# Attention scores on one core: three hand-kept 32 KB buffers in place of a rotating tile pool

## The chip, the core and the metric

The kernel runs on one core of a Trainium2 chip. The metric is the device time of one execution in microseconds, lower is better.

## The reference

```python
batch, heads, seq, dim = 8, 8, 512, 64          # q, k: float32
scale = 1.0 / np.sqrt(q.shape[-1])
out = (np.einsum('bhqd,bhkd->bhqk', q, k) * scale).astype(np.float32)
```

16.78 MB go in, 67.11 MB come out, and the arithmetic between is small.

## The kernel before

The work is cut into four units of two batches. Each unit loads k and q as fp32 into one 32 KB-per-partition tile (two loads of 2.1 MB), GpSimd casts them to bf16, TensorE transposes them, and VectorE and ScalarE copy the transposes to `kT` and `qz`. Then four output tiles per unit follow: sixteen matmuls into PSUM, eight evictions of 128 x 1024 with the scale (`n_evac % 6` deals them out, half to each engine), and one store of 4.2 MB. Input tiles and output tiles come from the same pool of three.

```python
    big_pool = ctx.enter_context(tc.tile_pool(name="big", bufs=3))
    ...
    def evacuate(dst, src):
        nonlocal n_evac

        if n_evac % 6 in (0, 2, 3):
            pinned(nc.scalar.mul(out=dst, in_=src, mul=scale))
        else:
            pinned(nc.vector.tensor_scalar(out=dst, in0=src, scalar1=scale, scalar2=None,
                                           op0=mybir.AluOpType.mult))
        n_evac += 1
    ...
    def load_and_cast(v):

        xf = big_pool.tile([P, 2, 2, J * D], f32, name="big")
        both = []
        for x, src in enumerate((k_r, q_r)):
            nc.sync.dma_start(out=xf[:, x], in_=src[v].rearrange("p (s c) -> p s c", s=2))
        for x in range(2):
            xb = bf_pool.tile([P, J, 2, D], bf16, name="xb")
            for s in range(2):
                pinned(nc.gpsimd.tensor_copy(out=xb[:, :, s, :],
                                             in_=xf[:, x, s].rearrange("p (j d) -> p j d", j=J)))
            both.append(xb)
        return both
    ...
    def scores(v, t):

        kT, qz = ts[v]
        o = big_pool.tile([P, 2, RO, S], f32, name="big")
        for x in range(2):
            n = 2 * t + x
            for i in range(0, RO, 2):
                ps = psum_pool.tile([P, 2, S], f32, name="ps")
                for w in range(2):
                    pinned(nc.tensor.matmul(out=ps[:, w, :], lhsT=qz[:, i + w, n, :],
                                            rhs=kT[:, n].rearrange("d m s j -> d (m s j)"),
                                            start=True, stop=True))
                evacuate(o[:, x, i:i + 2, :], ps)
                yield
        nc.sync.dma_start(out=out_r[v, t], in_=o.rearrange("p x i k -> p x (i k)"))
```

(Cuts are marked with `...`; the transposes, their copies and the main loop, which interleaves the transposes of the next unit with the scores of this one, are left out.)

## Time and profile before

| | before |
|---|---|
| time, median of three runs | 203.24 us (202.83 to 203.37) |
| span of the profiled run | 201.3 us |
| VectorE, ScalarE, TensorE busy | 126.4, 100.7, 99.2 us |
| DMA queue, share of 16 engines | 98.1% |
| moved | 83.89 MB |

(In the lines of profiles, PE is TensorE, DVE VectorE, ACT ScalarE, POOL GpSimd, and SP the engine that issues the DMAs; a q behind a name is that engine's sequencer, under which the waits stand, as with the 33 event semaphores of VectorE quoted below.)

The table answers one question: is any resource full? Only the DMA is. VectorE is busy 63% of the time, and the longest of its waits is for the queue: evictions waited 29.1 us on VectorE and 30.8 us on ScalarE for old stores to land. So the idle columns of the groups matter less here than the row of DMA shares. Two things are not on the page and had to be worked out from the trace: when each store is issued, and how many bytes stand in the queue at that moment (bytes issued before, less bytes moved). The second is called the backlog below. It is the time by which a store may be late before the DMA starves: the same 7.35 us of delay cost 5.5 us where the backlog was 3.2 us and 0.4 us where it was 9.3 us, as the second experiment shows.

### The profile page before, as it was taken

The numbers are of one execution on the slowest core, as the hardware profiler recorded it, in microseconds if no ns is written. First come the engines' busy times: TensorE is split into PE (matmuls) and PEld (weight loads), VectorE is DVE, ScalarE is ACT, GpSimd is POOL, SyncE is SP. The second block draws the span as 40 slices with busy tenths as digits, with TensorE's granted clock in tenths as the row PEclk, the third lists the DMA queues.
The fourth block names the chain that finished last, engine by engine and source line by source line (L and its number), as shares of the span: only waits on it lengthen the run. The fifth ranks groups of instructions, "written<-read, shape, count | busy, mean of one in ns | idle before, by whom it ended". The sixth has DMA issues, their size and how long they took to land.

```text
span 201.3 us, 1456 instructions
## 1 busy us (share of the span) xinstructions
PE 99.2 (49%) x503; PEld 48.3 (24%) x512; DVE 126.4 (63%) x130; ACT 100.7 (50%) x129; POOL 30.6 (15%) x22
## 2 busy tenths in 40 slices
PE   0033366753976729463729554856535666710000
PEld 0033353321522414231315221432212222200000
DVE  6726659995989929796749796569635264530000
ACT  2016667786674856583837663856515341510000
POOL 1277777556000000000000000000000000000000
PEclk9999999998599996999975998888995857555555
DMA  6999999999999999999999999999999999999993
GB/s 205 430 443 430 420 433 440 420 407 427 433 436 425 422 443 427 430 423 440 430 423 433 433 430 427 440 430 423 433 436 430 410 446 433 420 423 433 433 427 163
DMA packets 5510, 83.97 MB, mean 417 GB/s; under 512 B 384, under 2 KB 384, under 8 KB 384
## 3 DMA queue, kind: packets, MB, share of 16 engines
q1 hardware_dynamic: 5504, 83.89, 98.1%
q8 instruction: 4, 0.07, 0.1%
q14 instruction: 2, 0.02, 0.0%
HBM read 16.78 MB, written 67.11 MB: 417 GB/s over the span
## 4 chain that ended last, share of the span: by engine, by line
DMA 63%; DVE 16%; PE 3%; POOL 3%; ACT 1%; POOLq 1%; issue 1%; SPq 0%; DVEq 0%; ACTq 0%
DMA out_dram<-big 43%; DMA big<-in_q_dram 20%; DVE big L66 12%; PE ps L132 3%; DVE qz L95 3%; POOL xb L82 3%; DVE kT L95 1%; ACT big L64 1%; POOLq L186 1%; SPq L78 0%; DVEq L66 0%; SPq L137 0%; ACTq L64 0%; POOLq L82 0%
## 5 line engine op out<-in xcount | busy, mean ns | idle before, releaser
L132 PE MATMUL ps<-kT,qz 128*128 128x512 bf16 x247 | 81.1, 450 | 55.1 <-ACT big L64 39.2
L66 DVE TENSOR_SCALAR big<-ps 128x1024 f32<-128x1024 f32 x64 | 76.3, 1222 | 39.9 <-DMA out_dram<-big 29.1
L64 ACT ACTIVATE big<-ps 128x1024 f32<-128x1024 f32 x64 | 63.7, 1023 | 57.0 <-DMA out_dram<-big 30.8
L132 PEld LDWEIGHTS <-qz 128*128 128x128 bf16 x256 | 27.5, 111 | 96.0 <-issue 83.2
L82 POOL CAST xb<-big 128x2048 bf16<-128x2048 f32 x16 | 29.9, 1896 | 17.6 <-DMA big<-in_k_dram 11.9
L95 DVE COPY kT<-tp 64x512 bf16<-64x512 bf16 x32 | 22.0, 687 | 6.3 <-PE tp L107 5.7
L95 ACT COPY kT<-tp 64x512 bf16<-64x512 bf16 x32 | 18.5, 578 | 14.7 <-PE tp L107 14.4
L95 DVE COPY qz<-tp 64x512 bf16<-64x512 bf16 x32 | 22.0, 687 | 3.1 <-PE tp L116 2.7
L95 ACT COPY qz<-tp 64x512 bf16<-64x512 bf16 x32 | 18.5, 578 | 3.9 <-PE tp L116 3.6
L107 PE MATMUL tp<-identity,xb 128*128 128x128 bf16 x128 | 12.0, 254 | 16.5 <-POOL xb L82 12.5
L116 PE MATMUL tp<-identity,xb 128*128 128x128 bf16 x128 | 12.8, 265 | 6.0 <-DVE kT L95 3.5
L107 PEld LDWEIGHTS <-xb 128*128 128x128 bf16 x128 | 10.5, 116 | 20.8 <-POOL xb L82 12.8
L116 PEld LDWEIGHTS <-xb 128*128 128x128 bf16 x128 | 11.3, 122 | 10.9 <-issue 8.9
L147 DVE MEMSET qz<- 128x4096 uint32 x2 | 6.9, 3472 | 2.5 <-PEq L175 1.7
L95 ACT ACT_TABLE_LOAD x1 | 1.3, 1283 | 0.7 <-PEq L175 0.7
masks.py:199 POOL TENSOR_SCALAR_AFFINE_SELECT identity<-identity 128x128 bf16<-128x128 bf16 x1 | 0.3, 294 | 0.1
masks.py:197 POOL MEMSET identity<- 128x128 bf16 x1 | 0.2, 205 | 0.3 <-POOLq L175 0.3
L175 POOL MEMSET const-float32-0.0<- 128x1 f32 x1 | 0.1, 99 | 0.2 <-issue 0.2
L175 POOL MEMSET const-bfloat16-1.0<- 128x1 bf16 x1 | 0.1, 102 | 0.0
L175 POOL MEMSET const-uint8-127<- 128x1 uint8 x1 | 0.1, 102 | 0.0
L175 POOL MEMSET const-float32-1.0<- 128x1 f32 x1 | 0.1, 99 | 0.0
## 6 DMA issues: line engine op xcount, KB each, us to landing
out_dram<-big SPq DMA_DIRECT2D x16, 4096.0 KB, 21.4
big<-in_k_dram SPq DMA_DIRECT2D x4, 2048.0 KB, 19.2
big<-in_q_dram SPq DMA_DIRECT2D x4, 2048.0 KB, 24.2
```

The costliest lines, as they stand in the source:

```text
L64: pinned(nc.scalar.mul(out=dst, in_=src, mul=scale))
L66: pinned(nc.vector.tensor_scalar(out=dst, in0=src, scalar1=scale, scalar2=None, op0=mybir.AluOpType.mult))
L82: pinned(nc.gpsimd.tensor_copy(out=xb[:, :, s, :], in_=xf[:, x, s].rearrange("p (j d) -> p j d", j=J)))
L95: pinned(copy(out=dst(s, h), in_=src[:, h]))
L107: pinned(nc.tensor.transpose(out=tp[:, j, :], identity=identity, in_=kb[:, j0 + j].rearrange("p s d -> p (s d)")))
L116: pinned(nc.tensor.transpose(out=tp[:, i, jj, :], identity=identity, in_=qb[:, RO * jj + i0 + i].rearrange("p s d -> p (s d)")))
L132: pinned(nc.tensor.matmul(out=ps[:, w, :], lhsT=qz[:, i + w, n, :], rhs=kT[:, n].rearrange("d m s j -> d (m s j)"), start=True, stop=True))
L147: nc.vector.memset(qz, 0.0)
L175: nc = _bacc.Bacc("TRN2", target_bir_lowering=False, num_devices=1)
L186: with _tile.TileContext(nc) as tc:
```

## The change

The intent was to drop the pool's bookkeeping: three persistent buffers are taken once and handed out in turn. What changes with it is the grain of the waits. A tile of a pool waits until the whole earlier tile is done with; a persistent buffer is tracked by overlapping bytes, and has a history for each of them.

```diff
-    big_pool = ctx.enter_context(tc.tile_pool(name="big", bufs=3))
...
+    n_big = 0
+
+    def next_big():
+
+        nonlocal n_big
+        n_big += 1
+        return bigs[(n_big - 1) % 3]
+
     def load_and_cast(v):
 
-        xf = big_pool.tile([P, 2, 2, J * D], f32, name="big")
+        xf = next_big().rearrange("p (x s c) -> p x s c", x=2, s=2)
...
-        o = big_pool.tile([P, 2, RO, S], f32, name="big")
+        o = next_big().rearrange("p (x i k) -> p x i k", x=2, i=RO)
...
+    bigs = [consts.tile([P, 2 * RO * S], f32, name=f"big{n}") for n in range(3)]
     cast = [load_and_cast(v) for v in range(UNITS)]
```

## The prediction

> **What bounds the kernel now.** I read the page of the kernel before from the top: busy shares, slices, DMA queues, chain, groups. Then I asked for the timeline of the issuing engine and for the windows. First the busy shares and the slices (tenths of each of 40 slices of about 5 us):
>
> ```profile
> PE 99.2 (49%) x503; PEld 48.3 (24%) x512; DVE 126.4 (63%) x130; ACT 100.7 (50%) x129; POOL 30.6 (15%) x22
> ...
> DMA  6999999999999999999999999999999999999993
> GB/s 205 430 443 430 420 433 440 420 407 427 433 436 425 422 443 427 430 423 440 430 423 433 433 430 427 440 430 423 433 436 430 410 446 433 420 423 433 433 427 163
> ```
>
> No compute engine is above 63%. The DMA row is 9 in every slice but the first and the last, and the rate sits between 407 and 446 GB/s throughout. The part on DMA queues says the same in one number:
>
> ```profile
> q1 hardware_dynamic: 5504, 83.89, 98.1%
> ```
>
> One queue carries 83.89 MB (16.78 read, 67.11 written), and its packets fill 98.1% of the 16 engines' span of 201.3 us: 197.5 us. So 3.8 us per engine is all that better feeding of the DMA could ever return, and most of that is the ramp of the first slice and the drain of the last. Reading the packets one by one: the first starts at 1.75 us, the last ends at 200.1 us, and the time with eight or fewer of the 16 engines active is 2.2 us in all, every bit of it before 2 us or after 198 us.
>
> The waits confirm it from the other side. The waits by who ended them (total us, times, longest):
>
> ```profile
> ACT big L64 <- DMA out_dram<-big: 30.8, 11, 5.2
> ...
> DVE big L66 <- DMA out_dram<-big: 29.1, 11, 4.7
> ...
> POOL xb L82 <- DMA big<-in_q_dram: 5.7, 4, 2.2
> ...
> ACT big L64 <- POOL xb L82: 2.8, 2, 1.8
> ...
> DVE big L66 <- POOL xb L82: 2.1, 1, 2.1
> ```
>
> The first two lines are evictions (ACT and DVE, 11 of the 16 output tiles) that wait until an old store has left their buffer; the third is GpSimd's casts waiting for a load; the last two are evictions that wait for the casts of an input still in their buffer. The evictions wait about 60 us in all for stores to free their buffer. That is back-pressure from a full DMA queue and not a loss.
>
> The issues on the DMA's own queue tell how full it is (median us from issue to landing):
>
> ```profile
> out_dram<-big SPq DMA_DIRECT2D x16, 4096.0 KB, 21.4
> ```
>
> A store of 4.19 MB needs 9.8 us at 427 GB/s (the plateau of the slices), but takes 21.4 us from issue to landing, so usually more than one whole transfer stands ahead of it. For each store I subtracted the bytes moved by then from the bytes issued before it. The backlog at issue is 1.60 MB (3.8 us) at the first store (38.23 us), 2.54 MB at the second, 1.45 MB (3.4 us, the smallest) at the third (58.31 us), then 3.4 to 4.9 MB (8 to 11 us) for all others; at the last one (178.2 us) 10.5 us. After that issue the DMA needs 10.5 + 9.8 = 20.3 us, to about 199, as seen.
>
> [...] The trace has these: 33 on VectorE ahead of evictions, with a median of 49 ns, and 33 on ScalarE with 38 ns.
>
> **The change part by part.** Two things can differ: where the buffers lie, and which waits are derived.
>
> Placement. The built programs have the three buffers at the same three addresses, only the second and third swapped. The rotation is the same: inputs 0, 1, 2, 3 in buffers 0, 1, 2, 0, then outputs in 1, 2, 0, 1 and so on. Every engine's compute instructions come in the same order; the eight loads and sixteen stores have the same shapes and the same order on the same queue. Cost: 0. Bytes are unchanged, hence also the 197.5 us.
>
> Removed. A tile of a pool waits for the release of the whole earlier tile; a persistent buffer is tracked by the bytes that overlap. (a) The fourth k load waited for both loads of input 0 and all four casts; now for its k half alone. It was issued at 17.33 us, and the k casts end at 8.71 + 3.73 = 12.44 us, so it goes out about 4.8 us earlier. Backlog then: 14.9 us before it in the old kernel, so nothing lands earlier in a way that adds bandwidth. Path effect 0. (b) The first evictions into outputs 1 and 2 no longer wait for all casts of inputs 2 and 3, only for the casts of the bytes beneath: ACT gets back up to 2.8 us, DVE 2.1 us, both between 36 and 49 us. The third store, at 58.31 us, may go out up to 2 us earlier; the DMA had 3.4 us of work then. Path effect 0, but the thinnest reserve grows to perhaps 5 us.
>
> Added. The build shows event-semaphore instructions growing from 38 to 66 on VectorE and on ScalarE, and from 25 to 29 on the issuing engine. With persistent buffers each eviction after the first pass also waits for its own engine's eviction of the same bytes 24 evictions earlier (the eviction pattern has period 6, so it is always the same engine). Those are long over, before the store that must land anyway. Cost: 28 x 49 ns = 1.4 us on VectorE and 28 x 38 ns = 1.1 us on ScalarE, spread over about 140 us of evictions: some 0.1 us per output tile against a reserve of 8 us. Path effect 0.
>
> Sum: 203.24 + 0 + 0 + 0 = 203.2 us.
>
> **The rivals.** *Freed waits shorten the run.* For: DVE 12% and POOL 3% of the chain look like 15% to gain. Against: this chain follows a buffer's life, store, eviction, store; while it runs through VectorE the DMA is still busy with another store. Even if all of the early waits, some 2 us, counted, it would be 201.2, still within 2%. Only a shorter ramp or drain could give that, and the first six loads wait for nothing in both. *Added waits make VectorE the bound.* For: it is the busiest compute engine, and four evictions plus four to eight copies per output tile make 4 x 1.22 + 8 x 0.69 = 10.4 us at worst, beside 9.8 us for a store. Against: that holds only while copies run; over all, 126.4 us busy plus 1.4 is far below 197.5. [...] *The earlier load gets in the way of earlier ones.* All loads go down one queue[...]. The casts of those are needed only after 28 us. Perhaps 1 us on the third store's backlog, nothing on the end.
>
> **Range and chances.** With the mechanism at zero, what is left is spread: three runs before gave 202.83 to 203.37, which I take as the noise of one chip, and I widen it for another chip's DMA rate by about 0.2%. Range 202.5 to 203.9. Faster by over 2% would mean below 199.2, while the packets alone take 197.5 plus 1.75 of ramp and the 1.1 after the last packet, 200.4: as good as excluded, 1%. Slower by over 2% needs 4 us of an idle DMA; I leave 2% for a wait that I misread. Within 2%: 97%.
>
> **What would show it right or wrong.** In the profile of the changed kernel: DMA 9 in all inner slices and a queue share of 97.5 to 98.6%; the fourth k load issued near 12.5 us instead of 17.3; waits of DVE and ACT for casts down from 4.9 us to under 2; about 28 more event semaphores on each of both, with VectorE's busy time still 126 us; the waits of evictions for stores still near 60 us, or longer by what the casts gave back. The prediction is wrong if a slice in the middle drops below 400 GB/s, if the backlog at a store reaches zero, or if the plateau rate itself differs from 427 GB/s with the same packets.

(Three passages are cut from the record, as no trace or run of this case shows what they said of the hardware. No term of the sum is among them: it came to 203.24 + 0 + 0 + 0 = 203.2 us, and still does. Gone are a paragraph before "The change part by part", of which one sentence is left ("these" in it are event-semaphore instructions ahead of evictions); a supposition in the second rival, with the upper estimate that rested on it; and a supposition in the third. What the trace of the kernel before shows: 431, 430 and 429 GB/s in the windows from 46 to 92, to 138 and to 178 us, with compute engines at work, 403 from 0 to 46 us with the ramp, and 422 GB/s from 186 to 198 us with none at work. The first six loads landed one after another in the order of their issue, at 8.65, 13.52, 18.42, 23.32, 28.21 and 33.10 us. The third rival's "perhaps 1 us" is an estimate without a derivation. So is the 0.2% for another chip; the medians of the kernel before in the later rounds, on four chips, were 202.93 to 203.11 us.)

## The result

| | before | after |
|---|---|---|
| time, median of four runs each | 203.04 us | 203.12 us (202.90 to 203.41) |
| span of the profiled run | 201.3 us | 201.3 us |

The ratio is 1.0003, with a 95% interval of 0.9982 to 1.0024: the same. (Ratios here and below are the mean time of one kernel's fast runs over that of the other's of the same rounds, so not quite the ratio of the medians quoted.)

The page of the changed kernel, busy shares, DMA slices and DMA queue:

```profile
PE 100.7 (50%) x503; PEld 48.7 (24%) x512; DVE 126.3 (63%) x130; ACT 101.3 (50%) x129; POOL 30.6 (15%) x22
...
DMA  6999999999999999999999999999999999999993
...
q1 hardware_dynamic: 5504, 83.89, 98.2%
```

Nothing of weight moved: VectorE 126.3 against 126.4 us, the DMA slices digit for digit the same, the queue 98.2% against 98.1%.

The timeline of the issuing engine (start us, duration us, operation) shows the freed load. Before, the fourth pair of loads left together; after, the k load goes 5.1 us earlier:

```profile
17.33 0.33 SPq L78 DMA_DIRECT2D big<-in_k_dram  x1
17.70 0.43 SPq L78 DMA_DIRECT2D big<-in_q_dram  x1
```

```profile
12.21 0.33 SPq L84 DMA_DIRECT2D big<-in_k_dram  x1
17.12 0.33 SPq L84 DMA_DIRECT2D big<-in_q_dram  x1
```

The waits of the changed kernel, by who ended them, keep the back-pressure of the stores, and the two lines in which evictions waited for casts are gone from the list altogether:

```profile
ACT big L62 <- DMA out_dram<-big: 30.0, 12, 4.9
...
DVE big L64 <- DMA out_dram<-big: 28.8, 11, 4.8
...
POOL xb L88 <- DMA big<-in_q_dram: 4.5, 4, 1.2
```

The event semaphores ahead of VectorE's evictions, before and then after (duration ns min/median/max, first and last start):

```profile
L66 DVEq EVENT_SEMAPHORE  x33: 21/49/4258, 26.2 to 171.3; - x33
```

```profile
L64 DVEq EVENT_SEMAPHORE  x60: 21/21/5154, 25.9 to 175.2; - x60
```

In these two profiles the third store was issued at 57.01 us in place of 58.31, and its backlog was 1.92 MB (4.5 us) in place of 1.45 MB (3.4 us). How much of that is owed to the change is taken up with the delay in output tile 2 below: most of it is not. The first store went the other way, 38.81 us in place of 38.23, with 3.2 us of backlog in place of 3.8. The last packet ended at 200.1 us in both kernels.

One warning on the chain of waits. Its shares by engine, before and then after, at the same time within 0.1 us:

```profile
DMA 63%; DVE 16%; PE 3%; POOL 3%; ACT 1%; POOLq 1%; issue 1%; SPq 0%; DVEq 0%; ACTq 0%
```

```profile
DMA 46%; DVE 15%; PE 14%; ACT 6%; issue 4%; POOL 2%; DVEq 1%; ACTq 0%; SPq 0%
```

A reader of the second alone might think that the kernel had become less bound by the DMA and more by TensorE. Nothing of the kind happened. In the first 60 us the chain can follow the loads, or the casts and matmuls that wait for them, and a small shift can decide which. The chain says who was last at each step; it does not say who was full.

### The profile page after: what moved, and what is told of

Read it like the earlier page. It is cut to its first block, busy times and chain, and to the rows that moved or that the text cites. A ratio compares the mean times of both kernels' runs of the same rounds, so it can differ in the third digit from the quotient of the medians.

```text
span 201.3 us, 1516 instructions
## 1 busy us (share of the span) xinstructions
PE 100.7 (50%) x503; PEld 48.7 (24%) x512; DVE 126.3 (63%) x130; ACT 101.3 (50%) x129; POOL 30.6 (15%) x22
## 3 DMA queue, kind: packets, MB, share of 16 engines
q1 hardware_dynamic: 5504, 83.89, 98.2%
## 4 chain that ended last, share of the span: by engine, by line
DMA 46%; DVE 15%; PE 14%; ACT 6%; issue 4%; POOL 2%; DVEq 1%; ACTq 0%; SPq 0%
DMA out_dram<-big 43%; DVE big L64 10%; PE ps L138 9%; DMA big<-in_k_dram 4%; DVE kT L101 3%; PE tp L122 3%; ACT big L62 3%; PE tp L113 2%; DVE qz L101 2%; ACT qz L101 2%; POOL xb L88 2%; ACT kT L101 1%; DVEq L193 1%; ACTq L62 0%; DVEq L64 0%
## 5 line engine op out<-in xcount | busy, mean ns | idle before, releaser
L138 PE MATMUL ps<-kT,qz 128*128 128x512 bf16 x247 | 82.7, 458 | 54.0 <-ACT big L62 35.9
L64 DVE TENSOR_SCALAR big<-ps 128x1024 f32<-128x1024 f32 x64 | 76.3, 1221 | 39.7 <-DMA out_dram<-big 28.8
L138 PEld LDWEIGHTS <-qz 128*128 128x128 bf16 x256 | 28.2, 113 | 97.0 <-issue 86.5
L113 PEld LDWEIGHTS <-xb 128*128 128x128 bf16 x128 | 10.6, 117 | 20.4 <-POOL xb L88 12.5
```

Source lines behind the costliest of these rows:

```text
L113: pinned(nc.tensor.transpose(out=tp[:, j, :], identity=identity, in_=kb[:, j0 + j].rearrange("p s d -> p (s d)")))
```

## The experiments

**Theory.** From 2 us to the end the DMA never lacks work, so a wait removed or added elsewhere changes nothing until it exceeds the backlog. **Rivals.** VectorE stands on the chain with 15%, so its work counts; or the freed waits gained something and the added waits cost as much; or all of it is hidden whatever its size.

All runs are quoted as medians, with the kernel before of the same rounds beside them. Every result was correct except where it says that it was wrong.

### The DMA alone

```diff
-        for x in range(2):
-            xb = bf_pool.tile([P, J, 2, D], bf16, name="xb")
...
-        for x in range(2):
-            n = 2 * t + x
...                                  # casts, transposes, matmuls, evictions: all gone
         nc.sync.dma_start(out=out_r[v, t], in_=o.rearrange("p x i k -> p x (i k)"))
```

> Wrong results on purpose: the same eight loads and sixteen stores of the same three buffers in the same order, with no cast, transpose, matmul or eviction between them, so that the stores write the inputs. This is the DMA's part by itself. Theory (the DMA is the wall from 2 us to the end in both kernels): 203.1 us within 0.7, queue share 98 percent. Rival (compute or its waits cost the DMA something, by late stores or by contention): below 200 us, and what is below is what finer waits could ever win.

Measured: 201.37 us against 202.96, ratio 0.9936 (0.9918 to 0.9953). The values are wrong on purpose. The queue's line on the page of this run:

```profile
q1 hardware_dynamic: 5504, 83.89, 98.8%
```

With no computation at all the same transfers take 1.6 us less. That is outside the 0.7 us that I had allowed and 1.4 us above the rival's 200 us, so it lies between the two. What better feeding could win with these transfers in this order, in either kernel, is thus under 1% (0.6% by the ratio, 0.5 to 0.8%). By the cumulated bytes of the trace, the transfers are level with the changed kernel at 40 MB (both near 96 us), some 0.3 us ahead at 60 MB, 0.6 us at 80 MB and 1.1 us at 83.8 MB. Two things add up: the packets of 16 KB took 611.5 ns on average between 48 and 190 us, against 612.9 and 614.3 ns in the kernels before and after, and the drain was shorter (eight or fewer of the 16 engines at work for the last 0.4 us, against 2.1 and 1.7 us). Why is open. A deeper queue is not a sufficient reason, as the run with half tiles (last experiment) shows.

### The same delay at two places

The last eviction of one output tile is repeated six more times on VectorE, which changes no value and holds up that tile's store. In one kernel it is tile 0, whose store had 3.2 us of backlog; in the other tile 8, with 9.3 us.

```diff
                 evacuate(o[:, x, i:i + 2, :], ps)
+                if x == 1 and i == RO - 2 and (v, t) == (0, 0):      # second kernel: (2, 0)
+                    for _ in range(6):
+                        pinned(nc.vector.tensor_scalar(out=o[:, x, i:i + 2, :], in0=ps, scalar1=scale,
+                                                       scalar2=None, op0=mybir.AluOpType.mult))
```

> Theory (the DMA is the wall; a delay counts only where it exceeds the work still queued): the changed kernel with the last eviction of output tile 0 repeated six more times on VectorE, 6 x 1.225 = 7.35 us. In the profile of the changed kernel the first store had 3.2 us of queued DMA work ahead of it, so the DMA idles for about 4.1 us near 43 us and the time is 203.1 + 4.1 = about 207 us (206 to 208.5). Rival A (everything VectorE does on the chain counts): 203.1 + 7.35 = 210.5 us. Rival B (the early wait is hidden whatever it is): 203.1 us.

> The same six repeated evictions, 7.35 us of VectorE, but in output tile 8, whose store had 9.3 us of queued DMA work ahead of it. Theory: the DMA never idles, 203.1 us within 0.4. Rival A (work of VectorE on the chain counts wherever it stands): 210.5 us. Backlog at that store falls from 9.3 to about 2 us.

Measured: in tile 0, 208.63 us against 203.11 (ratio 1.0277, 1.0254 to 1.0300); in tile 8, 203.54 us against 203.11 (ratio 1.0021, 1.0002 to 1.0040). The DMA slices of the run with the delay in tile 0:

```profile
DMA  6999999909999999999999999999999999999995
```

The windows of the same run around the hole (stretch, length, busy us of PE, weight loads, VectorE, ScalarE, GpSimd, each with its count, then granted clock, DMA share, GB/s):

```profile
38.00:42.00 4.00, 1.40 (x12) 0.76 (x11) 3.90 (x4) 1.07 (x2) 2.73 (x2) 0.96 0.91 389
42.00:46.00 4.00, 0.44 (x1) 0.16 (x2) 3.93 (x4) 0.00 (x0) 2.87 (x3) 0.50 0.02 8
46.00:50.00 4.00, 2.04 (x6) 0.67 (x6) 3.89 (x6) 3.28 (x6) 1.87 (x2) 0.50 0.93 393
```

The page of the run with the delay in tile 8:

```profile
q1 hardware_dynamic: 5504, 83.89, 98.2%
```

One and the same 7.35 us of VectorE costs 5.5 us at the thin place, just above the 206 to 208.5 us that I had expected, and 0.4 us at the thick one. At the thin place the store left at 45.58 us, 6.8 us later than in the changed kernel; 3.2 us of that were covered, and the empty queue needed 0.9 us from the issue to its first packet (46.50 us), which I had not counted. 3.6 + 0.9 is 4.5 us, and the cumulated bytes show 4.4 us lost right behind the hole (at 17 MB), against the profile of the changed kernel. The rest, up to 5.5 us at 83.8 MB, came bit by bit: behind the hole a packet of 16 KB took 618 ns on average (70 to 190 us), against 614.5 ns in the changed kernel. The four runs with a hole at tile 2, below, show 618 to 619 ns behind it. Why packets stay slower is open. At the thick place the backlog at that store fell to 1.4 us and recovered over the next four stores to 11.0 us. The 0.4 us there touch the edge of what I expected; the profiled execution, with a span of 201.2 us, shows no hole.

### More work on VectorE, everywhere but early

The same edit, with two repeats in each of the output tiles 3 to 15.

> In output tiles 3 to 15 the last eviction is repeated twice more on VectorE: 26 x 1.225 = 31.9 us more work, VectorE 158 us busy of about 201 (79 percent). Theory: a tile then takes VectorE some 6.75 + 2.45 = 9.2 us on average against 9.8 us for a store, so the queue stays fed: 203.1 us within 0.5, and the waits of evictions for stores shrink from 29 us on VectorE to a few. Rival (the most used compute engine sets the time): up to 235 us. In between, if single tiles with many copies overrun: 204 to 207.

Measured: 206.13 us against 203.11 (ratio 1.0136, 1.0105 to 1.0166). VectorE was busy 157.5 us. The DMA slices:

```profile
DMA  6999999999999999999999989997979999999994
```

This is the "in between" of the expectation; the time lies 2.5 us above the upper end of my main guess. From the third store to the twelfth the issues came 10.5 us apart ((151.75 - 57.39) / 9), against 9.8 us that a store takes, so the backlog drained from 5.0 us at the fourth store to nothing at the eleventh and twelfth (140.61 and 151.75 us), where the two deeper dips stand (a first short one, at 120 us, is at the ninth). My average of 9.2 us of VectorE work per tile left out what a tile spends waiting for matmuls and for ScalarE, and was 1.3 us too low. The waits of VectorE's evictions for stores fell from 28.8 us to none. So of 31.9 us of added work all but 3 us vanished in waits that existed anyway. Note that VectorE's busy time, 157.5 us, is still far below the 197.5 us of the DMA: a comparison of busy times over the whole run does not show that an engine can keep the queue fed.

### Undoing the earlier load

A tiny load into the q half of buffer 0 stands ahead of the fourth k load on the queue, which issues in program order (15.40 and 15.79 us, below).

```diff
+        if v == UNITS - 1:
+            nc.sync.dma_start(out=xf[0:16, 1, 0, 0:128], in_=q_r[v][0:16, 0:128])
         for x, src in enumerate((k_r, q_r)):
```

> Undoes one freed wait: a tiny load of 8 KB into the q half of buffer 0, ahead of the fourth k load on the in-order queue, makes that k load wait for the q casts again (issue near 17.2 us in place of 12.2), and the q load two us later still. Theory: 20 us of loads are queued at that time, so nothing changes: 203.1 us within 0.4. Rival (the earlier load was worth its 4.9 us, and something else cost as much): 205 to 208 us.

Measured: 203.41 us against 203.11 (ratio 1.0017, 1.0002 to 1.0032). The timeline of the issuing engine (the tiny load, the k load, the q load):

```profile
15.40 0.34 SPq L84 DMA_DIRECT2D big<-in_q_dram  x1
15.79 0.42 SPq L86 DMA_DIRECT2D big<-in_k_dram  x1
33.27 0.33 SPq L86 DMA_DIRECT2D big<-in_q_dram  x1
```

The tiny load, at 15.40 us, waited for one q cast and not for both, as only half of q lies beneath it (in the trace of the changed kernel those casts end at 15.25 and 17.09 us), so the k load went at 15.79 us (12.21 without). The q load had to wait until the tiny one had landed at the back of a full queue (in the changed kernel the sixth load, which stands before it, landed at 32.87 us), and went at 33.27 us, 16 us later than without. That is a far harsher setback than I had meant, and the first store still left at 38.93 us (38.81) with 3.1 us of backlog (3.2). The 0.3 us are within the expectation and at the edge of the noise.

### The added waits, with VectorE as the bound

Where the DMA is the wall, the added waits can't show. So all 128 evictions go to VectorE, in both kernels.

```diff
-        if n_evac % 6 in (0, 2, 3):
+        if False:
```

> The kernel before with all 128 evictions on VectorE, so that VectorE and not the DMA is the wall: 126.4 + 64 x 1.225 = 204.8 us busy, from about 29 us on with 187 us to go, then 10 us for the last store: 225 to 235 us, DMA share under 92 percent. It is the base for the next run.

> The changed kernel with all evictions on VectorE. The build has 121 event-semaphore instructions on VectorE against 25 in the same kernel with the pool, 96 more. Theory (they wait for something 24 evictions old and pass while the engine still works on the one before): equal to the pool's version within 1 us, waits for casts aside (up to 2 us less). Rival (each takes its time on the engine): 96 x 21 to 49 ns = 2.0 to 4.7 us more than the pool's version.

Measured: 228.93 us with the pool and 228.99 us with the persistent buffers, beside a kernel before of 203.02 us (ratios 1.1277, 1.1255 to 1.1298, and 1.1278, 1.1257 to 1.1299). VectorE was busy 197.2 us in both (fewer than the 204.8 expected, as back-to-back evictions overlap a little: 128 of 1.216 us on average are 155.6 us, and they were busy 148.2), and the DMA queue was down to 87.6% and 87.2%. The event semaphores ahead of the evictions (duration ns min/median/max, first and last start), with the pool and then with the buffers:

```profile
L66 DVEq EVENT_SEMAPHORE  x20: 21/50/2331, 26.1 to 198.4; - x20
```

```profile
L64 DVEq EVENT_SEMAPHORE  x116: 21/21/1979, 26.1 to 207.2; - x116
```

96 more event semaphores, of which most pass in 21 ns, and no time: the rival's 2.0 to 4.7 us (0.9 to 2.0%) lie outside what the two intervals leave. The profiles agree to 0.01 us: from the issue of the first store to that of the last it took 168.62 us with the pool and 168.61 us with the buffers. The semaphores pass while the engine is still at earlier instructions: in the trace of the kernel before, one starts at 26.19 us, 18 ns after the start of a copy that runs until 26.86 us.

### The freed waits, with the queue run dry

The delay of the second experiment in output tile 2, the place where the freed waits should pay, in both kernels; then again with eight repeats.

> The kernel before with six repeated evictions (7.35 us of VectorE) at the end of output tile 2, whose store had 3.4 us of queued DMA work ahead of it. From the run with the same delay in tile 0, where 7.35 us less 3.2 us cost 5.5 us, the restart of an empty queue takes about 1.0 us on top (issue to first packet). Theory: 203.0 + 7.35 - 3.4 + 1.0 = about 208.0 us (206.5 to 209).

> The same delay in the changed kernel, whose third store had 4.5 us ahead of it, as its evictions no longer wait for the last casts. Theory: 1.1 us less than the same delay in the kernel before, about 206.9 us, which would show that the freed waits are real and become time once the queue runs dry. Rival (the freed waits only moved idle time about): equal within 0.4 us.

> Repeats the pair with the delay in output tile 2, as the first pair came out equal (207.96 and 208.15 us) although its two profiles stood 1.1 us apart: eight repeated evictions in place of six, in the kernel before. 2 x 1.225 = 2.45 us more, all of it past an empty queue: 208.0 + 2.45 = 210.4 us (209.8 to 211).

> The same eight in the changed kernel. If the freed waits are worth the 1.1 us of the profiles: 209.3 us, at least 0.7 us below the same delay in the kernel before. If they are not, because other things set the early tiles back as much (in the profiles of the changed kernel six to eight early matmuls ran at 631 to 634 ns in place of 378, between 30 and 33 us): 210.4 us, equal within 0.4 us.

Measured, against 202.96 us of the kernel before (six repeats) and 202.93 us (eight):

| | pool | persistent buffers |
|---|---|---|
| six repeats | 207.96 us, ratio 1.0259 (1.0237 to 1.0282) | 208.15 us, ratio 1.0265 (1.0248 to 1.0282) |
| eight repeats | 210.48 us, ratio 1.0378 (1.0355 to 1.0401) | 210.05 us, ratio 1.0346 (1.0323 to 1.0370) |

Two more repeats take 2.45 us on VectorE. They cost the pool's version 2.5 us and the other 1.9 us: past an empty queue nearly every microsecond counts. By the medians the pair differs by +0.2 us once and by -0.4 us once, with overlapping intervals. A gain of 1.1 us is not shown. The profiles suggest a reason. The wait of an eviction for the casts, in the pool's version, with six repeats and then with eight:

```profile
DVE big L66 <- POOL xb L82: 2.5, 1, 2.5
```

```profile
DVE big L66 <- POOL xb L82: 0.4, 1, 0.4
```

The wait itself changes from run to run, by 2.1 us here, and from two sides. The first are the first matmuls of the scores, from 29 to 34 us, in the same two runs (duration ns min/median/max):

```profile
L132 PE MATMUL ps<-kT,qz x12: 376/379/379, 29.9 to 33.4; 128*128 128x512 bf16 x12
```

```profile
L132 PE MATMUL ps<-kT,qz x10: 380/634/634, 30.1 to 33.9; 128*128 128x512 bf16 x10
```

Where they ran at 634 ns in place of 379, VectorE came to the buffer 0.7 us later (47.45 us in place of 46.74). The second, and the larger, are the casts of the last input, in the same two runs (start us, duration us):

```profile
45.45 3.73 POOL L82 CAST xb<-big 128x2048 bf16<-128x2048 f32 x2 [2.39 <-PE ps L132]
```

```profile
44.10 3.73 POOL L82 CAST xb<-big 128x2048 bf16<-128x2048 f32 x2 [0.98 <-DMA big<-in_q_dram]
```

With eight repeats they were done 1.35 us sooner, as the load beneath them had landed sooner (43.95 us in place of 45.30, by the landings in the trace). Of the 13 profiles with casts, these started at 45.0 us or later in the three whose first store left by 38.24 us, the kernel before among them, and by 44.3 us in the ten others. Why is open.

For the matmuls, the number of slow ones differs between runs of the same work: between 29 and 34 us none was slow in the profiles of the kernel before and of the pool's six repeats, nine in that of the pool's eight repeats; six in that of the changed kernel, eight in that of its six repeats, four in that of its eight. The granted clock reads 1.00 in this stretch on the pages of all of them, but this says nothing here: it is taken as full until the first entry of the clock's log, and that entry stands at 28.3 us in the kernel before and at 32.7 us in the changed one. In this stretch the slow matmuls end there: the last of 634 ns starts at 27.2 us in the kernel before, the last of 631 ns at 32.1 us in the changed one. What makes them slow is not shown. Over all 13 profiles, slow ones stand in seven of the eight of the changed kernel's versions and in one of the five of the pool's. These are too few to decide whether the change itself has a part in it.

So two profiles of these kernels can differ by a microsecond near the third store for reasons other than the freed waits. With six repeats that store left at 66.24 us (pool) and 65.14 us (buffers), and this profile of the pool is of the slowest of its five runs (209.28 us; the others took 207.77 to 208.01). With eight repeats the two profiles are alike at the start (first store at 38.94 and 38.87 us), and the third store left at 67.40 and 67.13 us: 0.3 us apart. What the freed waits give is below what nine or ten runs a side can tell from nothing. These links rest on the profiles alone; the timed runs beside them have none.

### The fine grain from a pool

The pool again, with six tiles of 16 KB, and each half of an output tile with a store of its own.

```diff
-    big_pool = ctx.enter_context(tc.tile_pool(name="big", bufs=3))
+    big_pool = ctx.enter_context(tc.tile_pool(name="big", bufs=6))
...
-        xf = big_pool.tile([P, 2, 2, J * D], f32, name="big")
+        xf = [big_pool.tile([P, 2, J * D], f32, name="big") for _ in range(2)]
...
-        o = big_pool.tile([P, 2, RO, S], f32, name="big")
         for x in range(2):
+            o = big_pool.tile([P, RO, S], f32, name="big")
...
-        nc.sync.dma_start(out=out_r[v, t], in_=o.rearrange("p x i k -> p x (i k)"))
+            nc.sync.dma_start(out=out_r[v, t][:, x], in_=o.rearrange("p i k -> p (i k)"))
```

> Tiles from the pool again, but cut in halves: six of 16 KB in place of three of 32 KB, and each half stored by its own DMA of 2.1 MB. This gives the finer waits without buffers kept by hand, and the first store can go after four evictions. Theory: first store near 35 us instead of 38 to 39, more queued work ahead of the early stores, but the bytes are the same: 203.1 us within 0.5. Rival (the early waits cost time that the changed kernel did not fully win back): 200 to 202 us. If 16 more DMAs cost something each on the queue: up to 204.

Measured: 204.13 us against 203.02 (ratio 1.0059, 1.0046 to 1.0071), slower by 1.1 us and clear of noise. The first store left at 32.75 us with 9.2 us of backlog, and the backlog grew to 17 to 19 us, so the reserve is as large as one could wish. It bought nothing. Nor was the time lost store by store: at 83.5 of the 83.9 MB this run is 0.1 us behind the kernel before (197.6 against 197.5 us), and the last packet ends 1.2 us later (201.26 against 200.09 us). The loss lies in the drain, the very end, when only some of the 16 engines still work. Why it is longer is open. The queue's line:

```profile
q1 hardware_dynamic: 5760, 83.89, 97.5%
```

256 more packets (sixteen small ones for each store), the same bytes, a lower share of a longer span. Of the versions tried none beats the two kernels, and the run of the DMA alone leaves under 1% to any that would keep these transfers in this order.

## Why the prediction was right

The time was predicted at 203.2 us (202.5 to 203.9) and measured at 203.12. Point by point:

- **"The bound is the DMA."** Shown, and with a size: the transfers alone take 201.4 us. The prediction's own floor, 200.4 us from packets, ramp and tail, is wrong in two ways, though the range did not suffer. It is a span, and was compared with a limit in device time (199.2 us), which is 1.8 us longer than the span in these runs (203.03 against 201.25 us in the profile before). And it is no floor: in spans, the transfers alone took 199.5 us, 0.9 us less. The share of packet time was 1.01 between 46 and 138 us, so packets of one engine overlap, and 100% is not its limit. The drain, too, was seen at 200.1 us and not at 199.
- **"Path effect 0" of the earlier load.** It went at 12.21 us, predicted near 12.5. Pushing its pair back again, the k load by 3.6 us and the q load by 16 us, cost 0.3 us (0.0 to 0.7 by the interval).
- **"Path effect 0" of the freed waits.** The waits for casts fell from 4.9 us to none (predicted: under 2), the third store went 1.3 us earlier (up to 2), the backlog there grew to 4.5 us (perhaps 5). That these two sizes fit is partly luck: in the pair of profiles that are alike at the start the third stores are 0.3 us apart. Even where the queue was made to run dry, the gain was not seen.
- **"Path effect 0" of the added waits.** 27 more event semaphores ran on each of the two engines ahead of evictions (60 against 33). Their price was put too high: the median is 21 ns on VectorE and 17 on ScalarE, not 49 and 38, since those medians had real waits in them. With VectorE as the bound, 96 of them cost nothing that could be measured.
- **The reserve.** The reading that a delay counts only beyond the backlog was shown by the pair of delays, 5.5 us at one place and 0.4 us at another. What the working lacked was the restart of an empty queue, 0.9 us, and the slower packets behind a hole (618 against 614.5 ns).
- **Not foreseen.** The first store left 0.6 us later than before. The matmuls at 631 ns from 30 to 32 us in that profile go with it. The kernel with the pool shows the same where its matmuls are slow (38.94 us, with eight repeats in a later tile), so it is not bound to the change; but slow matmuls stand in seven of eight profiles of the changed kernel's versions and in one of five of the pool's, so that the change has no part in it is not shown.
- **The rivals.** That VectorE becomes the bound was brought about by force: two more evictions in each of 13 tiles, 31.9 us in all, starve the DMA and cost 3 us. Less was not tried, so where it begins is not known. The prediction's argument that 127.8 us busy is far below 197.5 gave the right answer here, but 157.5 us already starved the queue. That the earlier load disturbs earlier ones was not seen: the first six loads landed 0.2 to 0.3 us sooner than in the kernel before (the first at 8.40 us in place of 8.65, the sixth at 32.87 in place of 33.10).

Still open are the cause of the 1.6 us between the transfers alone and the kernels, why packets stay slower behind a hole, and whether the freed waits are worth a few tenths in some runs.

## What to carry to other kernels

When one resource has work from the first microsecond to the last, count the backlog in front of it at each hand-over, in microseconds: in these runs, neither removed nor added waits below that number changed the time beyond noise, and above it nearly each microsecond counted, with the restart of the queue on top. Waits on something long past cost nothing here even where VectorE set the time (228.99 us with 96 more of them, 228.93 without), so with a full queue, buffers kept by hand and pool tiles can be chosen by what is easier to read. Don't expect finer transfers that free buffers sooner to help if the queue is already full: here they made the run 1.1 us longer. And before a difference between two profiles is put down to a change, compare profiles that were alike until then.

## Three more figures of the DMA

- One core, streaming alone, held 429 GB/s between 6 and 195 us, in the kernel before and in the changed one.
- From the start of an issue to the first packet it took 0.9 us on an emptied queue (five runs at 0.88 to 0.92) and 1.0 us at the start of the kernel (0.74 to 1.75 us). The issue of a store itself takes 0.37 to 0.40 us of that.
- At the start of the kernel the first twenty packets of 16 KB took up to 1.8 us each, against 0.61 later.
